# A decoder trunk on one core: first chunks made one by one, half of the last head's filler blocks put behind its values, first parts of the last feed-forward sooner

## The chip, the cores and the metric

The kernel runs on one core of a Trainium2 chip. The time is device microseconds (us) of one execution, the median of three runs. The engines have short names in the profile: PE (TensorE, matrix products), DVE (VectorE), ACT (ScalarE), POOL (GpSimd), SP (SyncE, which here only starts transfers). Each works through its own list of instructions in order, and they wait for each other by semaphores.

## The reference

Sequence 1024, model width 1024, one gated-convolution layer with a feed-forward, a shared compressed K/V, and one latent-attention layer (8 heads) with a feed-forward:

```python
h = h + short_conv_mixer(rms_norm(h, conv_norm_g[i]), conv_w_in[i], conv_w[i], conv_w_out[i])
h = h + swiglu_ffn(rms_norm(h, conv_ffn_norm_g[i]), conv_ffn_w13[i], conv_ffn_w2[i])
...
k_nope, k_pe, v = shared_mla_kv(h, kv_norm_g, w_dkv, kv_latent_norm_g, w_ukv, cos, sin)
...
p = jax.nn.softmax(jnp.where(mask, sc, neg), axis=-1).astype(v.dtype)
return jnp.einsum('bhqk,bkhd->bqhd', p, v)          # causal, in blocks of 128 queries
...
return attn.reshape(b, s, N_HEADS * V_HEAD_DIM) @ w_o
...
return rms_norm(h, final_norm_g)
```

## The kernel before

**Products.** Each float32 operand is split into a rounded high part (a cast on ACT, `split`, L111) and the rest (a subtraction on DVE or POOL, L112). A product is then three matmuls: high by high, high by low, low by high (`three`, L153 to L155; `gemm`, L146 to L150). So whatever PE multiplies has first passed one ACT and one DVE instruction.

**Order.** The convolution and both feed-forwards are written as steps of PE (`Steps`): `before(n, fn)` puts `fn` ahead of step n in the text, and the engines keep that order. The attention is written as plain code; there the Tile framework's scheduler sets each engine's order when the program is built, out of its own estimates.

**Start.** `first_x` loads four blocks of the input, transposes them raw, makes the norm, scales the first 512 columns (`scaled`, L919 and L921), and makes the operand of the first product: four chunks of 128 input columns by 512 tokens. `first_halves` makes chunks 0 and 1 (transposes, eviction with the gain at L952 and L954, split), `first_block(0, 1)` makes chunks 2 and 3 as one tile of 1024 columns: evictions at L932 and L934, one cast (L316), one subtraction (L317). Then the engines store the last raw block (L904), split the second weight (L378, L382) and scale the other columns; PE's first product (12 matmuls `q`) is followed by 16 transposes of those other columns.

**Attention.** For each head, eight `scores` blocks of 128 queries (PE `ps_s`, then on DVE the mask and the maximum, L1470 to L1473, on ACT the exponential, L1476, on DVE the division, L1478), and twice `pv`: transposes `ps_t` of p, their split into `pt` (L111, L112), and the values `ps_pv` (L1500 to L1502). The second `pv` of a head is kept in `pend` until the next head's blocks. PSUM holds two tiles of two banks (`ps2`, for `ps_s` and `ps_wo`) and four of one (`ps1`).

**Filler.** Between the scores of heads 0 to 6 PE makes the next head's keys and queries. Head 7 has no next head; there `project_o(O0, 0, (n,))` is put in, for n = 0 to 7: the output projection of the first five heads for one block of 128 output columns, 30 matmuls `ps_wo`. A block loads its weights (`wo_raw`, SP), splits them (`wo_hi` on ACT, `wo_lo` on POOL), loads the stream `h` from memory (L1549), and adds (L1552, DVE), which frees its `ps2` tile. `per` says after which pair of scores each block is written: two blocks after each pair. The last three heads' weights (`wo_r`, L1567) and their split (`wo_h`, `wo_l`) belong to the product that follows.

**Last feed-forward.** `Plain` adds heads 5 to 7 (`pl`, then `h` at L597). `Boundary.first(steps, n, at)` makes the norm of the first 512 tokens and, at the four steps of `at`, the first four operand parts (`Operand.first`, `block`: two instructions L301). Each call of `Operand.advance` moves the earlier parts one stage on: cast (L316), then subtraction (L317). `up(steps, quads2, bd.op, ahead)` makes the products `q`; `ahead` says how many steps sooner than usual the first two weights are split (L378, L382).

Of the kernel before, what the change touches and what calls it, by code (L numbers as in the profile page):

```python
# [9 lines left out]
F32 = mybir.dt.float32  # L10
F32R = mybir.dt.float32r
I32 = mybir.dt.int32
AF = mybir.ActivationFunctionType
ALU = mybir.AluOpType
AX = mybir.AxisListType

P = 128
S = 1024
D = 1024
KD = D // P  # L20
# [28 lines left out]
def trunk(ctx, tc, aps, out):  # L49
    nc = tc.nc  # L50
# [6 lines left out]
    def enter(name):  # L57

        if "stack" in phase:
            phase["stack"].close()  # L60
        phase["stack"] = ExitStack()
        phase["pool"] = phase["stack"].enter_context(tc.tile_pool(name=name, bufs=1, reuse_waits="tile"))
# [13 lines left out]
    def slot(name, dt=F32, shape=None):  # L76
        return slots.tile(shape or [P, S], dt, name=name, tag="act", bufs=NSLOT)
# [24 lines left out]
    def ps1(name):  # L102
        return phase["psum"].tile([P, 512], F32, name=name, tag="ps1", bufs=phase["ps"][1])
# [5 lines left out]
    def split(hi, lo, src, gain=None, eng=None):  # L109
        if gain is None:  # L110
            nc.scalar.copy(out=hi, in_=src)  # L111
            (eng or nc.vector).tensor_tensor(lo, src, hi.bitcast(F32), ALU.subtract)  # L112
        else:
            nc.scalar.activation(hi, src, AF.Copy, scale=gain)
            nc.vector.scalar_tensor_tensor(lo, src, gain, hi.bitcast(F32), ALU.mult, ALU.subtract)
# [42 lines left out]
    ident = const.tile([P, P], F32, name="ident")  # L158
# [25 lines left out]
    def gcol(nm, k):  # L184
        return vec[:, col[nm] + k:col[nm] + k + 1]
# [170 lines left out]
    class Quad:  # L356
# [88 lines left out]
        def evict(self, name):  # L445

            b = self.bank[name]
            add = lambda o, a: nc.vector.tensor_tensor(o, b, a, ALU.add)  # L448
            if name == 1:
                self.C1 = work("c1")  # L450
                nc.scalar.copy(out=self.C1[:, 512:], in_=b)
            elif name == 2 and name in self.onto:
                nc.scalar.activation(self.C1[:, :512], b, self.first)
            elif name == 2:
                add(self.C1[:, :512], self.C1[:, 512:])
                if self.first != AF.Copy:
                    nc.scalar.activation(self.C1[:, :512], self.C1[:, :512], self.first)
            elif name == 5:
                self.C2 = work("c2")
                nc.scalar.activation(self.C2[:, :512], b, AF.Copy, scale=-1.0)  # L460
                if 6 not in self.onto:
                    nc.vector.tensor_tensor(self.C1[:, 512:], self.C1[:, 512:], b, ALU.subtract)
            elif name == 6:
                nc.vector.tensor_tensor(self.C1[:, 512:], self.C1[:, 512:], b, ALU.subtract)
            elif name == 7:
                nc.vector.scalar_tensor_tensor(self.C2[:, 512:], b, -1.0, self.C1[:, 512:], ALU.mult, ALU.subtract)
                nc.vector.tensor_tensor(self.C2[:, :512], self.C2[:, :512], self.C2[:, 512:], ALU.add)
            elif name == 4:
                nc.vector.tensor_tensor(self.C2[:, :512], self.C2[:, :512], b, ALU.subtract)
            else:  # L470
                add(self.C1[:, 512:], self.C1[:, 512:])
                if self.first != AF.Copy:
                    nc.scalar.activation(self.C1[:, 512:], self.C1[:, 512:], self.first)  # L473
# [381 lines left out]
    steps = Steps()  # L855
    xt = [None] * KD
    xop = Operand("conv_norm_g")
# [80 lines left out]
    def first_block(f, kk):  # L938
        xop.part((f, 0), kk, block(f, 0, kk, nc.vector))
        xop.advance()  # L940

    def first_halves():

        b, hi, lo = slot("xraw"), slot("xh", F32R), slot("xl", F32R)
        pts = [ps1("xps") for _ in range(2)]
        for c, pt in enumerate(pts):
            for tb in range(4):
                nc.tensor.transpose(pt[:, tb * P:(tb + 1) * P], xt[tb][:, c * P:(c + 1) * P], ident)
        for c, pt in enumerate(pts):
            o = slice(c * 512, (c + 1) * 512)  # L950
            if c == 0:
                nc.vector.tensor_scalar(b[:, o], pt, gcol("conv_norm_g", c), None, ALU.mult)  # L952
            else:
                nc.scalar.activation(b[:, o], pt, AF.Copy, scale=gcol("conv_norm_g", c))  # L954
            split(hi[:, o], lo[:, o], b[:, o])
        xop.raw.setdefault((0, 0), {})[0] = b
        xop.X.setdefault((0, 0), {})[0] = (hi, lo)

    def first_x():
        for tb in range(3):  # L960
            raw_x(tb)
        squares(*range(4))
        last = raw_turn(3)
        gains(0)
        norms(0)
        conv_quads[0].pair_hi()
        scaled(0, slice(0, 512))
        conv_quads[0].pair_lo()
        first_halves()
        first_block(0, 1)  # L970
        xop.advance()
        raw_store(3, last, (nc.vector, nc.scalar))
        conv_quads[1].pair_hi()
        scaled(0, slice(512, S))
        conv_quads[1].pair_lo()
# [105 lines left out]
    quads2 = ffn_quads(A["mla_ffn_w13"], md["f2"])  # L1081
# [6 lines left out]
    n0 = len(steps.pe)  # L1088
# [392 lines left out]
    def pv(V, g, ps_, h):  # L1481

        nb = 4 * g + 4
        o = ps1("ps_pv")
        PT = {}

        def turn(kb):
            c = slice(max(kb - 4 * g, 0) * P, 512)
            t = ps1("ps_t")
            for j in range(c.start // P, 4):  # L1490
                nc.tensor.transpose(t[:, j * P:(j + 1) * P], ps_[j][:, kb * P:(kb + 1) * P], ident)  # L1491
            pt = hi_tile("pt")
            PT[kb] = pt[:, :512], pt[:, 512:]
            split(PT[kb][0][:, c], PT[kb][1][:, c], t[:, c])

        def product(kb):
            c = slice(max(kb - 4 * g, 0) * P, 512)
            vh, vl = [t[:, kb % 4 * 256 + h % 2 * P:kb % 4 * 256 + h % 2 * P + P] for t in V[kb // 4]]
            th, tl = [t[:, c] for t in PT[kb]]
            nc.tensor.matmul(o[:, c], lhsT=vh, rhs=th, start=kb == 0, stop=False)  # L1500
            nc.tensor.matmul(o[:, c], lhsT=vh, rhs=tl, start=False, stop=False)
            nc.tensor.matmul(o[:, c], lhsT=vl, rhs=th, start=False, stop=kb == nb - 1)  # L1502

        for kb in range(nb + 2):
            if kb < nb:
                turn(kb)
            if kb >= 2:
                product(kb - 2)
        gs = slice(g * 512, (g + 1) * 512)
        if h in Od:  # L1510
            split(Od[h][0][:, gs], Od[h][1][:, gs], o)
            return
        oh, ol = (pslot("oh", "oh", 1, F32R, [P, 512]), pslot("ol", "ol", 1, F32R, [P, 512]))
        split(oh, ol, o)
        move(od[h, 0, :, gs], oh)
        move(od[h, 1, :, gs], ol)
# [57 lines left out]
    for h in range(H):  # L1574
        if h >= 6:
            Od[h] = (tmp("oth", dt=F32R), tmp("otl", dt=F32R))
        if h + 1 < H:
            jobs = [lambda h=h: make_k(h + 1), lambda h=h: make_q(h + 1)]
            if h % 2:
                jobs = [lambda: make_qr(h + 1), lambda: make_v(h + 1)] + jobs  # L1580
        else:
            O1 = [load_o(5, r_(), r_())] + [Od[6], Od[7]]
            jobs = [lambda n=n: project_o(O0, 0, (n,)) for n in range(KD)]
        if h == 0:
            jobs = [lambda: make_q(1)]
        per = {1: ((0,), (), (), ()), 2: ((), (0,), (1,), ()), 4: ((0,), (1,), (2,), (3,)), 8: ((0, 1), (2, 3), (4, 5), (6, 7))}[len(jobs)]
        p = []
        for i in range(4):
            if i == 2 and pend:
                pv(*pend.pop(0))  # L1590
            p += [scores(Kt[h], Qt[h], 2 * i + d) for d in range(2)]
            if i == 2:
                pv(Vt[h], 0, p[:4], h)
            if i == 3:
                pend.append((Vt[h], 1, p[4:], h))
            for j in per[i]:
                jobs[j]()
        if h == 6:
            r_ = lambda: slot("oth", F32R)
            O0 = [load_o(k, r_(), r_() if k < 3 else cq_tile(4 - k)) for k in range(5)]  # L1600
# [2 lines left out]
    wo_parts(5)  # L1603
    for u in pend:
        pv(*u)
    enter("ffn")
    enter_psum(0, 8)

# [4 lines left out]
        steps.before(j, lambda k=k: wo_parts(k))  # L1613
    pl = Plain(steps, None, [[5], [6], [7]], Kept(O1), bd.norm.add, wo_kept)
    e = pl.ends
    bd.first(steps, e[1] + 2, (e[1] + 4, e[1] + 5, e[1] + 7, e[1] + 8))
    bd.second(steps, e[3] + 1)
    n0 = up(steps, quads2, bd.op, 8)
    for j, fn in enumerate(sums):
        paced(steps, n0 + 2 + 13 * j // 4, fn)  # L1620

# [114 lines left out]
```

## Time and profile before

| | |
|---|---|
| median of three runs | 2098.05 us (2097.63 to 2100.79) |
| the profiled execution | 2095.82 us |
| its span in the trace | 2093.7 us |
| busy share of the span | PE 98%, DVE 70%, ACT 41%, POOL 13% |
| matmuls | 9542 |

The page says that PE is busy in 98% of the span. So the time is PE's own work plus the places where it waits, and only those places and the clock can give anything. They are read from PE's list of instructions in order of time, where a bracket holds the idle time ahead of an instruction and what ended it.

### The profile page before, as it was taken

What the parts mean: (1) busy time and instruction counts of PE and PEld (TensorE: products, weight loads), DVE (VectorE), ACT (ScalarE), POOL (GpSimd) and SP (SyncE); (2) the same over time, 40 slices, a digit from 0 to 9 for tenths busy, and PEclk for the clock granted to TensorE, in tenths of its full rate; (3) what the DMA queues carried; (4) which work ended last, traced back from release to release, by engine and by line L of the source; (5) the groups of instructions that cost most, each with busy time, mean ns of one, the idle gap of its engine ahead of it and who ended that gap; (6) DMA issues with size and microseconds to landing.
All of it is one profiled execution on the core that took longest, in us unless ns stands there. A gap on an engine that the chain in (4) does not pass through costs nothing.

```text
span 2093.7 us, 25560 instructions
## 1 busy us (share of the span) xinstructions
PE 2053.9 (98%) x9542; PEld 1704.7 (81%) x9542; DVE 1463.5 (70%) x2200; ACT 855.7 (41%) x1440; POOL 269.4 (13%) x388
## 2 busy tenths in 40 slices
PE   7999999999999999999999999989999999999998
PEld 6888888888888887787888888867888888888887
DVE  5996666787667668867577777437887666667556
ACT  7533433533333333354245455225433333333455
POOL 1111100121122110000023322101111111100000
PEclk9999999999999999999999999999999999999999
DMA  7355765596766586554232213425487565686553
GB/s 234 81 133 139 238 239 175 112 220 180 190 163 153 141 287 246 206 206 150 72 70 70 66 52 111 163 81 163 125 201 186 154 160 163 151 286 225 186 169 129
DMA packets 274316, 338.97 MB, mean 162 GB/s; under 512 B 18047, under 2 KB 177984, under 8 KB 273872
## 3 DMA queue, kind: packets, MB, share of 16 engines
q1 hardware_dynamic: 240144, 262.71, 38.8%
q0 software_dynamic: 33888, 74.56, 16.6%
q8 instruction: 74, 1.21, 0.2%
q14 instruction: 50, 0.41, 0.1%
q10 hardware_dynamic: 160, 0.07, 0.0%
HBM read 260.22 MB, written 126.35 MB: 185 GB/s over the span
## 4 chain that ended last, share of the span: by engine, by line
PE 88%; DVE 6%; ACT 2%; issue 2%; DMA 1%; DVEq 0%; SPq 0%; ACTq 0%
PE q L154 17%; PE q L155 17%; PE q L153 17%; PE dn L155 5%; PE dn L153 5%; PE dn L154 5%; PE ps_s L1469 4%; PE pl L153 2%; PE pl L155 2%; PE pl L154 2%; DVE wp_lo L112 1%; PE ps_t L1491 1%; PE ps_l L155 1%; PE ps_l L153 1%; PE ps_l L154 1%
## 5 line engine op out<-in xcount | busy, mean ns | idle before, releaser
L153 PE MATMUL q<-xh,w_hi 128*128 128x512 f32 x1568 | 612.4, 391 | 1.1 <-ACT xh L316 1.1
L154 PE MATMUL q<-xl,w_hi 128*128 128x512 f32 x1568 | 610.5, 389 | 2.3 <-DVE xl L317 2.1
L155 PE MATMUL q<-xh,w_lo 128*128 128x512 f32 x1568 | 610.4, 389 | 0.0
L154 PEld LDWEIGHTS q<-xl,w_hi 128*128 128x128 f32 x1568 | 294.4, 188 | 64.6 <-DVE xl L317 2.8
L153 PEld LDWEIGHTS q<-xh,w_hi 128*128 128x128 f32 x1568 | 294.3, 188 | 63.3 <-ACT xh L316 1.5
L155 PEld LDWEIGHTS q<-xh,w_lo 128*128 128x128 f32 x1568 | 294.3, 188 | 61.0
L112 DVE TENSOR_TENSOR w_lo<-wr,w_hi 128x512 fp32r<-128x512 f32 (+1 forms) x272 | 191.9, 705 | 199.3 <-ACT w_hi L111 197.5
L111 ACT CAST w_hi<-wr 128x512 fp32r<-128x512 f32 (+1 forms) x272 | 170.4, 630 | 293.5 <-DVE wr L390 191.2
L155 PE MATMUL dn<-mp_hi,wp_lo 128*128 128x512 f32 (+1 forms) x628 | 243.9, 388 | 2.6 <-DVE wp_lo L112 0.8
L153 PE MATMUL dn<-mp_hi,wp_hi 128*128 128x512 f32 (+1 forms) x628 | 242.9, 387 | 0.0
L154 PE MATMUL dn<-mp_lo,wp_hi 128*128 128x512 f32 (+1 forms) x628 | 242.0, 385 | 0.0
L1072 POOL COPY paced<-pace 128x1 f32<-128x1 f32 x128 | 75.1, 587 | 1020.4 <-ACT pace L1071 1020.4
L112 DVE TENSOR_TENSOR mp_lo<-m,mp_hi 128x1024 fp32r<-128x1024 f32 x84 | 95.2, 1134 | 120.4 <-ACT mp_hi L111 120.4
L111 ACT CAST mp_hi<-m 128x1024 fp32r<-128x1024 f32 x84 | 82.4, 980 | 221.7 <-PE dn L154 211.5
L155 PEld LDWEIGHTS dn<-mp_hi,wp_lo 128*128 128x128 f32 x628 | 117.9, 188 | 32.7 <-DVE wp_lo L112 9.6
L154 PEld LDWEIGHTS dn<-mp_lo,wp_hi 128*128 128x128 f32 x628 | 118.0, 188 | 23.6
L153 PEld LDWEIGHTS dn<-mp_hi,wp_hi 128*128 128x128 f32 x628 | 118.0, 188 | 23.0 <-DVE h L740 0.2
L112 DVE TENSOR_TENSOR wp_lo<-w,wp_hi 128x1024 fp32r<-128x1024 f32 x84 | 94.8, 1128 | 0.0
L111 ACT CAST wp_hi<-w 128x1024 fp32r<-128x1024 f32 x84 | 82.1, 977 | 0.0
L473 ACT ACTIVATE c<-c 128x512 f32<-128x512 f32 x44 | 27.8, 632 | 131.7 <-DVE c L448 131.7
L1476 ACT ACTIVATE p<-ps_s,mx,rq 128x128 f32<-128x128 f32 (+3 forms) x64 | 53.2, 833 | 55.3 <-DVE mx L1473 50.1
L382 DVE TENSOR_TENSOR w_lo<-wr,w_hi 128x1024 fp32r<-128x1024 f32 x56 | 68.2, 1218 | 7.9 <-ACT w_hi L378 7.9
(296 smaller groups left out, 3231.9 us busy)
## 6 DMA issues: line engine op xcount, KB each, us to landing
m<-md_f SPq DMA_DIRECT2D x70, 512.0 KB, 4.9
md_f<-c SPq DMA_DIRECT2D x110, 256.0 KB, 3.7
wr<-in_conv_ffn_w_dram SPq DMA_DIRECT2D x47, 512.0 KB, 6.3
wr<-in_mla_ffn_w_dram SPq DMA_DIRECT2D x47, 512.0 KB, 5.4
w<-mw_f SPq DMA_DIRECT2D x40, 512.0 KB, 3.9
h<-hd SPq DMA_DIRECT2D x32, 512.0 KB, 9.6
wr<-in_conv_w_in_dram SPq DMA_DIRECT2D x31, 512.0 KB, 5.7
mw_f<-in_conv_ffn_w_dram POOLq DMA_DIRECT2D x30, 512.0 KB, 7.7
```

The lines of the kernel that those rows point to most:

```text
L111: nc.scalar.copy(out=hi, in_=src)
L112: (eng or nc.vector).tensor_tensor(lo, src, hi.bitcast(F32), ALU.subtract)
L153: nc.tensor.matmul(ps, lhsT=wh, rhs=xh, start=st, stop=False, **more)
L154: nc.tensor.matmul(ps, lhsT=wh, rhs=xl, start=False, stop=False, **more)
L155: nc.tensor.matmul(ps, lhsT=wl, rhs=xh, start=False, stop=en, **more)
L382: nc.vector.tensor_tensor(lo, self.ra, hi.bitcast(F32), ALU.subtract)
L473: nc.scalar.activation(self.C1[:, 512:], self.C1[:, 512:], self.first)
L1072: nc.gpsimd.tensor_copy(b, a)
L1469: nc.tensor.matmul(ps[:, a:b], lhsT=q[:, qs], rhs=k[:, a:b], start=i == 0, stop=i == 4)
L1476: nc.scalar.activation(p[:, :kw], ps[:, :kw], AF.Exp, bias=mx, scale=rq[:, qb:qb + 1], accum_out=rsum)
L1491: nc.tensor.transpose(t[:, j * P:(j + 1) * P], ps_[j][:, kb * P:(kb + 1) * P], ident)
```

## The change

At the start, `first_chunks` takes the place of `first_halves` and `first_block(0, 1)`: all sixteen transposes first, then for each of four chunks an eviction, a cast and a subtraction of 512 columns, woven by hand. In head 7, `per` writes one block of the projection after each pair of scores, and the other four (n = 4 to 7) are written after the last values. In the last feed-forward, the four operand parts come at e[1] + 4, 4, 5, 7, with one more `advance` at e[1] + 6, and `ahead` is 10.

```diff
-    def first_halves():
-        b, hi, lo = slot("xraw"), slot("xh", F32R), slot("xl", F32R)
-        pts = [ps1("xps") for _ in range(2)]
...
+    def first_chunks():
+        pts, T = [], [[slot("xraw"), slot("xh", F32R), slot("xl", F32R)] for _ in range(2)]
+        at = lambda k: [t[:, k % 2 * 512:k % 2 * 512 + 512] for t in T[k // 2]]
+        for k in range(4):
+            pts.append(ps1("xps"))
             for tb in range(4):
+                nc.tensor.transpose(pts[k][:, tb * P:(tb + 1) * P], xt[tb][:, k * P:(k + 1) * P], ident)
...
+        for fn, k in ((evict, 0), (high, 0), (evict, 1), (low, 0), (high, 1), (evict, 2), (low, 1), (high, 2), (evict, 3),
+                      (low, 2), (high, 3), (low, 3)):
+            fn(k)
...
         conv_quads[0].pair_lo()
-        first_halves()
-        first_block(0, 1)
-        xop.advance()
+        first_chunks()
...
-        per = {..., 8: ((0, 1), (2, 3), (4, 5), (6, 7))}[len(jobs)]
+        per = {..., 8: ((0,), (1,), (2,), (3,))}[len(jobs)]
...
     for u in pend:
         pv(*u)
+    for j in range(4, KD):
+        jobs[j]()
...
-    bd.first(steps, e[1] + 2, (e[1] + 4, e[1] + 5, e[1] + 7, e[1] + 8))
+    bd.first(steps, e[1] + 2, (e[1] + 4, e[1] + 4, e[1] + 5, e[1] + 7))
+    steps.before(e[1] + 6, bd.op.advance)
...
-    n0 = up(steps, quads2, bd.op, 8)
+    n0 = up(steps, quads2, bd.op, 10)
```

`evict` uses DVE for even chunks and ACT for odd ones, `high` is the cast on ACT, `low` the subtraction on DVE.

**Start, ACT's list.** These are ACT's instructions from the scaled input (`xt`) to the next scaled input; `xps` are the transposed chunks, `xraw`, `xh`, `xl` the operand and its parts. Before, then after:

```order
L919 ACTIVATE xt<-xt,rs 128x512 x2
L111 CAST xh<-xraw 128x512
L954 ACTIVATE xraw<-xps,vec 128x512
L111 CAST xh<-xraw 128x512
L934 ACTIVATE xraw<-xps,vec 128x512
L316 CAST xh<-xraw 128x1024
L904 COPY xr<-xps 128x512
```

```order
L959 CAST xh<-xraw 128x512
L953 ACTIVATE xraw<-xps,vec 128x512
L959 CAST xh<-xraw 128x512 x2
L953 ACTIVATE xraw<-xps,vec 128x512
L959 CAST xh<-xraw 128x512
```

The cast of 1024 columns has become two of 512, and the one of chunk 2 stands ahead of the eviction of chunk 3.

**The last values, PE's list.** Before, the last head's values stood alone behind the last block of the projection, each waiting for the `pt` that ACT and DVE make from the transposes just ahead:

```order
L150 MATMUL ps_wo<-oth,wo_lo 128x512 x2
L1491 MATMUL ps_t<-ident,p 128x128 x3
L1500 MATMUL ps_pv<-pt,vh 128x512
L1501 MATMUL ps_pv<-pt,vh 128x512
L1502 MATMUL ps_pv<-pt,vl 128x512
L1491 MATMUL ps_t<-ident,p 128x128 x4
```

After, the last transposes stand ahead of block 4 of the projection, whose last rows and the first values are these:

```order
L146 MATMUL ps_wo<-oth,wo_hi 128x512 x2
L148 MATMUL ps_wo<-cq,wo_hi 128x512
L1511 MATMUL ps_pv<-pt,vh 128x512
L148 MATMUL ps_wo<-cq,wo_hi 128x512
L150 MATMUL ps_wo<-oth,wo_lo 128x512 x2
L1512 MATMUL ps_pv<-pt,vh 128x512
```

The values lie among the matmuls of the projection's blocks 4 to 6, and block 7 comes behind them all. On DVE, the last two score blocks of head 7 now read like this (mask, maximum `mx`, the split of `wo_l`, the scaled maximum for which ACT's exponential waits):

```order
L1481 TENSOR_TENSOR ps_s<-ps_s,cmask 128x128
L1483 TENSOR_REDUCE mx<-ps_s 128x1
L112 TENSOR_TENSOR wo_l<-wo_r,wo_h 128x1024
L1484 TENSOR_SCALAR mx<-mx,nrq 128x1
L1481 TENSOR_TENSOR ps_s<-ps_s,cmask 128x128
```

Before, that split stood behind the second of the two maxima. SP's list of loads for the same stretch, as the piece of the difference:

```order
-L127 DMA wo_raw<-in_mla_w_o_dram 128x5x128 x5
-L1549 DMA h<-hd 128x1024 x4
-L127 DMA wo_raw<-in_mla_w_o_dram 128x5x128 x3
+L127 DMA wo_raw<-in_mla_w_o_dram 128x5x128 x4
+L1578 DMA wo_r<-in_mla_w_o_dram 128x1024
+L1560 DMA h<-hd 128x1024 x2
+L1578 DMA wo_r<-in_mla_w_o_dram 128x1024 x2
+L1560 DMA h<-hd 128x1024 x5
+L127 DMA wo_raw<-in_mla_w_o_dram 128x5x128
```

The weights of blocks 4 to 7 of the projection, four loads in all, now stand behind loads of `h`: seven ahead of block 4's.

**The last feed-forward, DVE's list.** From the norm's diagonal (`dg`) on; `h<-h,pl` adds the projection. Before, then after:

```order
L597 TENSOR_TENSOR h<-h,pl 128x512
L301 SCALAR_TENSOR_TENSOR xraw<-h,vec,R_12067 128x512 x2
L597 TENSOR_TENSOR h<-h,pl 128x512 x2
L301 SCALAR_TENSOR_TENSOR xraw<-h,vec,R_12067 128x512 x2
L597 TENSOR_TENSOR h<-h,pl 128x512 x4
L317 TENSOR_TENSOR xl<-xraw,xh 128x1024
```

```order
L301 SCALAR_TENSOR_TENSOR xraw<-h,vec,R_12069 128x512 x4
L597 TENSOR_TENSOR h<-h,pl 128x512 x2
L317 TENSOR_TENSOR xl<-xraw,xh 128x1024
L301 SCALAR_TENSOR_TENSOR xraw<-h,vec,R_12069 128x512 x2
L597 TENSOR_TENSOR h<-h,pl 128x512 x2
L317 TENSOR_TENSOR xl<-xraw,xh 128x1024
```

The first two parts are made together, and the first `xl` comes behind three additions where it came behind seven.

## Rows read from the trace of the kernel before

**Rows 1.** Windows: stretch, its length, busy time of each engine, granted PE clock, DMA

```profile
40.00:1100.00 1060.00, 1055.86 (x4731) 869.69 (x4730) 770.75 (x1067) 413.99 (x684) 125.74 (x189) 1.00 0.59 169
1450.00:2094.00 644.00, 636.61 (x2879) 527.27 (x2878) 442.08 (x605) 254.74 (x405) 61.00 (x88) 1.00 0.61 178
```

**Rows 2.** Timeline of PE at the start: start, duration, instruction, idle before

```profile
19.85 0.50 PE L153 MATMUL q<-xh,w_hi 128*128 128x512 f32 x1 [1.06 <-ACT xh L316]
21.11 0.50 PE L154 MATMUL q<-xl,w_hi 128*128 128x512 f32 x1 [0.76 <-DVE xl L317]
...
22.39 1.91 PE L929 MATMUL xps<-ident,xt 128*128 128x128 f32 x16
```

**Rows 3.** Timeline of ACT at the start

```profile
16.66 0.62 ACT L111 CAST xh<-xraw 128x512 fp32r<-128x512 f32 x1
17.18 0.68 ACT L934 ACTIVATE xraw<-xps,vec 128x512 f32<-128x512 f32 x1
18.75 1.04 ACT L316 CAST xh<-xraw 128x1024 fp32r<-128x1024 f32 x1 [0.89 <-DVE xraw L932]
...
21.12 1.34 ACT L919 ACTIVATE xt<-xt,rs 128x512 f32<-128x512 f32 x2
```

**Rows 4.** Timeline of DVE at the start

```profile
16.07 0.69 DVE L112 TENSOR_TENSOR xl<-xraw,xh 128x512 fp32r<-128x512 f32 x1 [0.68 <-ACT xh L111]
...
17.92 0.74 DVE L932 TENSOR_SCALAR xraw<-xps,vec 128x512 f32<-128x512 f32 x1
```

**Rows 5.** Timeline of PE in the last head and behind it

```profile
1317.11 0.51 PE L1500 MATMUL ps_pv<-pt,vh 128*128 128x512 f32 x1 [0.83 <-ACT pt L111]
1317.95 0.53 PE L1501 MATMUL ps_pv<-pt,vh 128*128 128x512 f32 x1 [0.33 <-DVE pt L112]
...
1372.63 0.60 PE L1491 MATMUL ps_t<-ident,p 128*128 128x128 f32 x4
1375.84 0.73 PE L1469 MATMUL ps_s<-kh,qnh 128*128 128x512 f32 x2 [2.61 <-ACT p L1476]
...
1382.32 1.22 PE L146 MATMUL ps_wo<-oth,wo_hi 128*128 128x512 f32 x2 [3.59 <-DVE h L1552]
...
1385.05 0.70 PE L146 MATMUL ps_wo<-oth,wo_hi 128*128 128x512 f32 x2
...
1386.51 0.62 PE L146 MATMUL ps_wo<-oth,wo_hi 128*128 128x512 f32 x2
...
1398.36 0.50 PE L1500 MATMUL ps_pv<-pt,vh 128*128 128x512 f32 x1 [0.46 <-ACT pt L111]
1399.49 0.50 PE L1501 MATMUL ps_pv<-pt,vh 128*128 128x512 f32 x1 [0.63 <-DVE pt L112]
```

**Rows 6.** Timeline of DVE ahead of PE's longest wait

```profile
1379.92 1.22 DVE L112 TENSOR_TENSOR wo_l<-wo_r,wo_h 128x1024 fp32r<-128x1024 f32 x1
1381.05 1.22 DVE L1552 TENSOR_TENSOR h<-ps_wo,h 128x1024 f32<-128x1024 f32 x1
```

**Rows 7.** Windows around the two longest waits; the clock is third from the end

```profile
1374.00:1376.00 2.00, 0.16 (x1) 0.16 (x2) 0.64 (x3) 1.19 (x2) 0.00 (x0) 1.00 0.64 231
...
1382.00:1384.00 2.00, 1.68 (x4) 1.39 (x5) 1.74 (x5) 1.29 (x2) 0.00 (x0) 0.50 0.97 315
```

**Rows 8.** Tile `wo_raw`: durations in ns, its split, issue to landing in us

```profile
L111 ACT CAST wo_hi<-wo_raw x7: 727/729/730, 1298.6 to 1370.4; 128x640 fp32r<-128x640 f32 x7
L112 POOL TENSOR_TENSOR wo_lo<-wo_raw,wo_hi x7: 1562/1566/1571, 1299.4 to 1371.2; 128x640 fp32r<-128x640 f32 x7
...
DMA to landing us min/median/max: 3.0/3.1/3.8
```

**Rows 9.** Tile `h` from 1300 to 1400 us: issue to landing

```profile
DMA to landing us min/median/max: 3.3/4.5/10.6
```

**Rows 10.** Timeline of PE at the last feed-forward's first norm and first product

```profile
1425.63 1.95 PE L224 MATMUL sp<-ones,nsq 128*128 128x1 f32 x16 [0.81 <-DVE nsq L759]
...
1445.18 0.51 PE L154 MATMUL q<-xl,w_hi 128*128 128x512 f32 x1 [1.32 <-DVE xl L317]
```

More of the change, by code (lines that the diff above doesn't have):

```diff
@@ L940, in first_block, with evict, high, low @@
         xop.advance()
-    def first_halves():
-        b, hi, lo = slot("xraw"), slot("xh", F32R), slot("xl", F32R)
-        pts = [ps1("xps") for _ in range(2)]
-        for c, pt in enumerate(pts):
-            for tb in range(4):
[L948 to L952, printed above, removed]
-            else:
[L954 to L957, printed above, removed]
+    def first_chunks():
[3 more added lines that the diff above has]
+            pts.append(ps1("xps"))
+            for tb in range(4):
+                nc.tensor.transpose(pts[k][:, tb * P:(tb + 1) * P], xt[tb][:, k * P:(k + 1) * P], ident)
+        def evict(k):
+            if k % 2:
+                nc.scalar.activation(at(k)[0], pts[k], AF.Copy, scale=gcol("conv_norm_g", k))
+            else:
+                nc.vector.tensor_scalar(at(k)[0], pts[k], gcol("conv_norm_g", k), None, ALU.mult)
+        def high(k):
+            b, hi, lo = at(k)
+            nc.scalar.copy(out=hi, in_=b)
+        def low(k):
+            b, hi, lo = at(k)
+            nc.vector.tensor_tensor(lo, b, hi.bitcast(F32), ALU.subtract)
+        for fn, k in ((evict, 0), (high, 0), (evict, 1), (low, 0), (high, 1), (evict, 2), (low, 1), (high, 2), (evict, 3),
+                      (low, 2), (high, 3), (low, 3)):
+            fn(k)
+        for kk, (b, hi, lo) in enumerate(T):
+            xop.raw.setdefault((0, 0), {})[kk] = b
+            xop.X.setdefault((0, 0), {})[kk] = (hi, lo)
     def first_x():
@@ L1585, in trunk @@
             jobs = [lambda: make_q(1)]
-        per = {1: ((0,), (), (), ()), 2: ((), (0,), (1,), ()), 4: ((0,), (1,), (2,), (3,)), 8: ((0, 1), (2, 3), (4, 5), (6, 7))}[len(jobs)]
+        per = {1: ((0,), (), (), ()), 2: ((), (0,), (1,), ()), 4: ((0,), (1,), (2,), (3,)), 8: ((0,), (1,), (2,), (3,))}[len(jobs)]
         p = []
```

## Prediction

> **What bounds the kernel now.** I read the windows first. From 40 to 1100 us PE is busy for 1055.86 of 1060 us, and from 1450 us to the end for 636.61 of 644 us [rows 1]. Long stretches are PE's own work, so whatever is saved ahead of them arrives at the end, and nothing on another engine counts unless PE waits for it. Then I read PE's timeline, with the reader looking only at the brackets. They lie in three places, and the change touches all three: the start, where the first product waits for its operand [rows 2]; the last head and the values behind it [rows 5]; and the first norm and first product of the last feed-forward [rows 10]. Last I read what ACT and DVE did ahead of those brackets [rows 3, 4, 6].
>
> **The start.** Nothing is removed; one tile of 1024 columns becomes two chunks of 512. Before, the first product waits 1.06 us for the cast of chunks 2 and 3 and 0.76 for their subtraction [rows 2], since that cast begins only at 18.75, behind both evictions, with ACT idle for 0.89 us [rows 3]. After, DVE's eviction of chunk 2 follows its first subtraction (16.07 + 0.69 = 16.76, then 0.74: 17.50) [rows 4], ACT casts it to 18.12 (0.62), evicts chunk 3 to 18.80 (0.68) and casts it to 19.42 (0.62) [rows 3]. The single cast ended at 18.75 + 1.04 = 19.79. Back to back, rows on ACT overlap by about 0.1 us (16.66 + 0.62 = 17.28 against the next start at 17.18) [rows 3], so 19.2 is nearer: ACT is 0.6 us ahead. PE itself would be some 1.8 us ahead, but its next work is 16 transposes of columns that ACT still has to scale. ACT does that from 21.12 to 22.46 [rows 3], so 0.6 us sooner. Before, the transposes began at 22.39 [rows 2] and met the last scaled block at once; after, three of each four are done while PE waits for the fourth, which gives back another 0.1 to 0.3. I take **0.8 us**, by ACT's chain, which is the longest here; the ends are 0 (ACT's later work in this stretch decides alone) and 1.8 (PE's own two waits).
>
> The split itself costs: two casts of 0.62 against one of 1.04 are 0.2 us more on ACT [rows 3]. That is in the 0.6 above, since ACT had 0.89 us of idle time to pay it from. [...]
>
> **The last head.** Four blocks of 30 matmuls move from between the scores to behind them; PE's work stays the same, and the waits change. Gone are:
> - 2.61 us ahead of the last scores, which waited for the exponential of the block before them to free a PSUM tile [rows 5]. The other tile was held by block 5, whose addition came late. With one block less at each place, the last scores take the tile of block 2, whose addition is done by then.
> - 3.59 us ahead of block 6, which waited for that addition at 1381.05, itself behind a maximum and a split of 1.22 us on DVE [rows 5, 6].
> - 0.46 and 0.63 us ahead of the last values, and 0.83 and 0.33 us ahead of the values at 1317 [rows 5]. PE now has matmuls of the projection between the transposes and the values that need them: at 1317 eight of them, about 1.9 us, at the end most of block 4.
> - the slow clock behind the long wait. [...] The wait of 2.61 us left the clock at 1.00 in its window [rows 7], so shorter waits cost only themselves.
>
> New is a wait of block 3 for the tile that the same exponential frees. Before, the tile was free 3.21 us after the transposes began (1372.63 to 1375.84) [rows 5]. After, DVE has a split of 1.22 us between the maximum and its scaling (its size is in [rows 6]), so 4.4 us; PE fills 0.8 of them with six transposes (0.60 for four) and 2.4 with ten score matmuls (1.46 / 6 each) [rows 5]: **1.2 us** remain. Its ends are 0 (the split slips behind) and 2.4 (a second split gets in between).
>
> The four blocks' loads hide as follows. Block 4's weights stand on SP behind loads of `h` that wait until the last scores have read their tiles. From the middle of those scores PE still has about 1.2 + 1.2 + 7.3 (30 matmuls of 0.24) + 0.8 us, some 10.5, before block 4. Against it stand 1.2 us of issuing three loads, a landing that I put at 5 (3.1 alone, 4.5 the median of `h` in company [rows 8, 9]), 0.73 of cast and 1.57 on POOL [rows 8]: 8.5. So 2 us are spare; with the longest landing, 10.6 [rows 9], it would be 3.6 late. Blocks 5 to 7 have a block more each.
>
> Sum here: 2.61 + 3.59 + 0.46 + 0.63 + 0.83 + 0.33 + 1.27 − 1.2 = **8.5 us**.
>
> **The last feed-forward.** With `ahead` at 10, both splits of the first weights (1.22 us each, as the same shape in [rows 6]) leave the run of additions and squares that ends in the norm, or reach its very beginning; the norm's matmuls waited 0.81 us for the end of that run [rows 10], so this wait goes with 0.4 us to spare even if only one split is out of its way. The wait of 1.32 us is for the subtraction of the second part [rows 10]. That part is now made with the first, one step sooner, and the added `advance` takes its cast and subtraction one step further forward: two steps of nine matmuls at 0.24, about 4.3 us. The third and fourth parts are needed only by later products. Both waits go: **2.1 us**. The ends are 0.8 and 2.1. DVE does no more than before, only in another order.
>
> **Sum.** 0.8 + 8.5 + 2.1 = 11.4 us. The profiled execution took 2095.82 us for its span of 2093.7, so it would take 2084.4; the median stands 2.2 us above the profiled one, and 2098.05 − 11.4 gives **2086.7 us**.
>
> **The rivals.**
> 1. Block 4 is late: its loads queue behind the loads of `h`. For it: the list of SP, and landings of up to 10.6 us in company [rows 9]. Against it: 2 us to spare. It would cost 2 to 4 us: 2089 to 2091.
> 2. The waits only move: the scores still hang on mask, maximum, exponential, and PE, with four blocks less between them, waits for each. In the first three pairs of scores PE now has half the filler, 7.3 us less. For it: the 2.61 us [rows 5] show what a missing filler costs, and two more such waits give back 5.2: 2092. Against it: the first pairs have the transposes and values of head 6 and then of head 7 around them in PE's list as well.
> 3. The change does nothing that lasts: the start and the head come sooner, and the last feed-forward waits for weights that now load later, behind the projection's. It would need 7 us or more of such waits: 2094 to 2099. Against it: PE is busy 99% from 1450 on [rows 1], and the first weights were split far ahead of use.
> 4. Slower: ACT's list has the casts of blocks 4 and 5 ahead of the casts of the last `pt`. If those weights come late, ACT stands, and with it the values, the softmax's rest and the next splits. It decides from a landing about 16 us beyond the 2 spare: then the 11.4 are gone and 4 more. That is longer than any landing in [rows 8, 9]; 2102 or more.
>
> **How the numbers follow.** The forecast, with terms within their ends (2085 to 2089), has 0.64; rival 1 has 0.14, rival 2 0.10, rival 3 0.06, rival 4 0.03; the remaining 0.03 is for more than forecast (the start's 1.8 in full, no wait at block 3), 2083 to 2085. A range from 2083 to 2091.5 holds the forecast, the better end and rival 1, 0.81. A measurement of this kernel can tell some 0.2%, 4.2 us, from no change. Faster by more than that is below 2093.9: forecast, better end and rivals 1 and 2, 0.90 with a little of rival 2 lost; the same 0.07; slower 0.03.
>
> **What would show it.** Right: in PE's timeline no bracket at the last values and none over 2 us between 1300 us and the last feed-forward, one of about 1.2 ahead of block 3, the clock at 1.00 there, no wait at the norm (`sp`) or at the first `q`, and the first transposes of the second operand at the start some 0.7 us sooner. Wrong: a bracket ahead of `wo_hi` of block 4 or `wo_lo` behind it, brackets at `ps_s` in the first pairs of head 7, or waits of the first `q` for `w_hi`.

## The result, and the profile after

The changed kernel takes 2084.97 us in the median of four runs (2083.35 to 2086.14). The ratio of its runs to those of the kernel before is 0.9928 (95% interval 0.9916 to 0.9940): 15.1 us faster (12.6 to 17.6) of 2098. The medians on record stand 12.9 us apart (2097.88 in four runs of the kernel before). The forecast was faster by 11.4 us, with 0.9 for its sign. The sign held, and the waits went where the forecast put them; the size did not hold: 2098.05 times the ratio is 2082.9, just below the range, though the median itself lies in it. The profiled execution took 2084.46 us for a span of 2082.7, 11.0 us less than the span of before; so the two profiles agree with the forecast, and the timed runs do not. That is the riddle that the experiments take up.

The long stretches are unchanged, as in [rows 1]. Windows of the kernel after:

```profile
40.00:1100.00 1060.00, 1055.98 (x4731) 869.66 (x4730) 770.52 (x1067) 414.09 (x684) 126.98 (x189) 1.00 0.59 169
1300.00:1395.00 95.00, 91.94 (x466) 76.74 (x465) 47.68 (x91) 32.87 (x61) 15.86 (x18) 1.00 0.46 153
...
1439.00:2083.00 644.00, 635.24 (x2872) 525.76 (x2870) 441.57 (x605) 253.28 (x403) 57.46 (x88) 1.00 0.61 178
```

PE's timeline of the kernel after, at the start, in the last head and at the last feed-forward (start, duration, instruction, idle before):

```profile
13.09 0.67 PE L949 MATMUL xps<-ident,xt 128*128 128x128 f32 x3 [2.20 <-DVE xt L921]
...
19.84 0.50 PE L154 MATMUL q<-xl,w_hi 128*128 128x512 f32 x1 [0.23 <-DVE xl L963]
...
20.84 0.77 PE L929 MATMUL xps<-ident,xt 128*128 128x128 f32 x3 [0.26 <-DVE xt L921]
...
36.84 0.77 PE L929 MATMUL xps<-ident,xt 128*128 128x128 f32 x5 [0.50 <-ACT xt L919]
...
1304.74 0.39 PE L1512 MATMUL ps_pv<-pt,vh 128*128 128x256 f32 x1 [0.57 <-DVE pt L112]
...
1353.73 0.73 PE L146 MATMUL ps_wo<-oth,wo_hi 128*128 128x512 f32 x2 [1.42 <-ACT p L1487]
...
1394.91 0.39 PE L153 MATMUL pl<-oth,wo_h 128*128 128x512 f32 x1
...
1413.73 0.40 PE L155 MATMUL pl<-oth,wo_l 128*128 128x512 f32 x1
1413.96 1.84 PE L224 MATMUL sp<-ones,nsq 128*128 128x1 f32 x16
...
1430.31 0.39 PE L153 MATMUL q<-xh,w_hi 128*128 128x512 f32 x1
...
1436.26 0.50 PE L153 MATMUL q<-xh,w_hi 128*128 128x512 f32 x1 [0.35 <-ACT c L451]
```

Where [rows 5] had waits of 2.61, 3.59, 0.46, 0.63, 0.83 and 0.33 us, one of 1.42 ahead of block 3 is left (forecast 1.2). The waits of [rows 10] at `sp` and at the first `xl` are gone; one of 0.35 for ACT's eviction of `c` is new. At the start 1.06 and 0.76 [rows 2] have become a few of about 0.25.

DVE ahead of block 3's wait shows the cause that was forecast: the split of `wo_l` stands between the maximum and its scaling.

```profile
1349.75 1.09 DVE L1483 TENSOR_REDUCE mx<-ps_s 128x1 f32<-128x896 f32 x1
1351.05 1.23 DVE L112 TENSOR_TENSOR wo_l<-wo_r,wo_h 128x1024 fp32r<-128x1024 f32 x1 [0.21 <-PE ps_s L1480]
1352.19 0.21 DVE L1484 TENSOR_SCALAR mx<-mx,nrq 128x1 f32<-128x1 f32 x1
```

The tile `wo_raw` of the kernel after, from 1352 us on: the four late loads land in 5.4 to 6.5 us (forecast 5), and ACT stands 3.2 us for block 4's, but PE has no bracket there:

```profile
  ACT wo_hi L111: 3.2, 1
...
DMA to landing us min/median/max: 5.4/5.4/6.5
```

### The profile page after: what moved, and what is told of

Its sections match the earlier page's. It is cut to its first block, busy times and chain, and to the rows that moved or that the text cites. A ratio compares the mean times of both kernels' runs of the same rounds, so it can differ in the third digit from the quotient of the medians.

```text
span 2082.7 us, 25559 instructions
## 1 busy us (share of the span) xinstructions
PE 2050.6 (98%) x9542; PEld 1701.2 (82%) x9542; DVE 1463.8 (70%) x2201; ACT 855.4 (41%) x1441; POOL 267.4 (13%) x388
## 4 chain that ended last, share of the span: by engine, by line
PE 88%; DVE 6%; ACT 3%; issue 2%; DMA 2%; DVEq 0%; SPq 0%; ACTq 0%
PE q L153 16%; PE q L155 16%; PE q L154 16%; PE dn L155 5%; PE dn L154 5%; PE dn L153 5%; PE ps_s L1480 4%; PE pl L155 2%; PE pl L153 2%; PE pl L154 2%; PE ps_t L1502 1%; DVE wp_lo L112 1%; PE ps_l L155 1%; PE ps_l L153 1%; PE ps_l L154 1%
## 5 line engine op out<-in xcount | busy, mean ns | idle before, releaser
L382 DVE TENSOR_TENSOR w_lo<-wr,w_hi 128x1024 fp32r<-128x1024 f32 x56 | 68.3, 1219 | 12.9 <-ACT w_hi L378 7.9
```

Source lines behind the costliest of these rows:

```text
L382: nc.vector.tensor_tensor(lo, self.ra, hi.bitcast(F32), ALU.subtract)
```

## The experiments

Two theories. **Theory 1**: the gain is the waits of the profile at their own price, and the rest is spread. **Theory 2**: the kernel before loses more in most executions than in the one that was profiled, at places that the change takes away; the profile had a lucky execution.

Three stretches of PE's timeline are compared in every profile, each as the difference of two starts. *Start*: from the first transposes of the scaled input (13.09 above) to the five transposes with the bracket of 0.50 (36.84). *Head*: from the values at 1304.74 to the first `pl`. *Norm*: from the last `pl` ahead of the sums `sp` to the first `q`. The same rows of the kernel before, from the profile that the prediction read:

```profile
13.28 2.17 PE L948 MATMUL xps<-ident,xt 128*128 128x128 f32 x8 [2.19 <-DVE xt L921]
...
37.86 0.77 PE L929 MATMUL xps<-ident,xt 128*128 128x128 f32 x5 [0.50 <-ACT xt L919]
...
1305.79 0.39 PE L1501 MATMUL ps_pv<-pt,vh 128*128 128x256 f32 x1 [0.58 <-DVE pt L112]
...
1405.54 0.45 PE L153 MATMUL pl<-oth,wo_h 128*128 128x512 f32 x1
...
1424.43 0.39 PE L155 MATMUL pl<-oth,wo_l 128*128 128x512 f32 x1
...
1442.08 0.39 PE L153 MATMUL q<-xh,w_hi 128*128 128x512 f32 x1
```

| profile | start | head | norm | timed ratio to before |
|---|---|---|---|---|
| before, as predicted from | 24.58 | 99.75 | 17.65 | |
| before_look1 | 24.57 | 102.29 | 19.19 | |
| before_look2 | 24.52 | 102.76 | 19.19 | |
| before_look3 | 25.45 | 101.20 | 19.19 | |
| start_only | 23.75 | 101.22 | 20.85 | 1.0005 (0.9996 to 1.0014) |
| ffn_only | 24.59 | 99.64 | 16.57 | 0.9979 (0.9971 to 0.9988) |
| before_filled | 24.58 | 99.67 | 17.64 | 0.9990 (0.9981 to 0.9999) |
| before_filled_look | 25.37 | 99.77 | 19.22 | |
| head_only | 25.68 | 90.19 | 19.25 | 0.9949 (0.9937 to 0.9962) |
| head_only_look | 24.58 | 90.18 | 17.64 | |
| head_filled | 24.59 | 90.19 | 17.64 | 0.9949 (0.9937 to 0.9962) |
| head_filled_look | 26.32 | 90.18 | 17.65 | |
| head_ffn | 24.54 | 90.22 | 16.57 | 0.9927 (0.9915 to 0.9940) |
| ahead8 | 23.76 | 90.44 | 19.23 | 0.9941 (0.9927 to 0.9955) |
| after | 23.75 | 90.17 | 16.58 | 0.9928 (0.9916 to 0.9940) |
| after_again | 23.75 | 90.18 | 16.58 | 0.9926 (0.9913 to 0.9938) |
| wo5_later | 23.76 | 89.72 | 16.58 | 0.9926 (0.9913 to 0.9940) |

**after_again** is the changed kernel, unedited.

> The changed kernel once more, to settle the size of the gain: the profiled pair differs by 11.4 us, the ratio of the timed runs says 15.1 (12.6 to 17.6). Theory 1 (the gain is the waits and the slow clock of the forecast, the rest is spread between executions): a ratio of about 0.9945 (11.4 us), its interval reaching over 11.4. Theory 2 (the kernel before loses about 3.5 us more in most executions than in the profiled one, at a place that the change takes away): 0.9928 again, 14 to 16 us, with an interval that leaves 11.4 out.

The ratio is 0.9926, 15.5 us (13.0 to 18.3): 11.4 lies outside, so theory 1 falls and the riddle is real.

**start_only, head_only, ffn_only** are the kernel before with one part of the diff each: `first_chunks`; `per` and the loop over `jobs[j]`; `bd.first`, `advance` and `ahead`.

> The kernel before with the new start alone. Theory 1: 0.8 to 1.1 us faster (the second product began 0.9 us sooner in the profile of the changed kernel), a ratio of 0.9995 to 0.9996. Theory 2, if its place is the start (granted clock 0.50 from 14 to 16 us before, 1.00 after): 3 to 5 us, 0.9976 to 0.9986. The rival that the start only moves a wait: 1.0000.

> The kernel before with four blocks of the projection behind the last head's values, alone. Theory 1: 8.3 to 8.5 us faster (the forecast's sum, a wait of 1.4 us for block 3 where 1.2 was forecast), a ratio of 0.9960; no bracket over 2 us between 1300 and 1400 us. Theory 2, if its place is the last head (the wait for block 5's addition and the clock behind it vary): 11.5 to 12.5 us, 0.994 to 0.9945. The rival that the waits only move: 3 us, 0.9985.

> The kernel before with the last feed-forward's first parts sooner, alone. Theory 1: 2.1 us faster less a small wait ahead of the first product (0.35 in the changed kernel's profile): 1.8 to 2.1, a ratio of 0.9990; the brackets of 0.81 at sp and 1.32 at the first xl are gone. Rival: without the head's change DVE and ACT are still behind with the last values there, so that one of the two waits stays: 0.8 to 1.3 us.

The head alone gave 10.7 us (8.0 to 13.2), with both answers to the question of size inside. The feed-forward gave 4.4 (2.5 to 6.1), more than its two waits. The start gave nothing in time (1.0 slower, from 2.9 slower to 0.8 faster), though its stretch is 0.8 shorter; one of its eleven runs took 2106.40, and by the medians it is 0.3 faster. This profile also has the longest norm.

**before_look1, before_look2, before_look3** are the kernel before, unedited.

> The kernel before again, for its profile: is the profiled execution of the prediction (sums sp to first q of the last feed-forward in 16.45 us, values at 1305.79 to first pl in 99.75) like the others? Theory 1: yes, both stretches within 0.2 us. Theory 2 (the clock falls behind the waits in most executions): sp to q 18.0 to 19.7, head 100 to 101.5 us.

> As before_look1, a second execution: by theory 1 the same figures as in the prediction's profile, by theory 2 at least one of the two stretches 1 us longer.

> A third further profile of the kernel before: stretch from the values at 1306 to the first pl 101 to 103 us and sp to q 18.0 or more by theory 2 (99.75 and 16.45 in the prediction's profile, which theory 1 takes as typical).

Theory 2 holds: heads 1.5 to 3.0 us longer (two of them beyond its 101.5) and norms 1.5 longer than in the profile behind the prediction. It is not a matter of the chip alone: start_only and ffn_only ran on one chip, with the same head, and read 101.22 and 99.64. PE's timeline of before_look1 shows how:

```profile
1376.04 1.22 PE L1469 MATMUL ps_s<-kh,qnh 128*128 128x512 f32 x2 [2.61 <-ACT p L1476]
1377.06 1.05 PE L1469 MATMUL ps_s<-kl,qnh 128*128 128x512 f32 x2
...
1383.95 1.22 PE L146 MATMUL ps_wo<-oth,wo_hi 128*128 128x512 f32 x2 [3.59 <-DVE h L1552]
...
1387.53 1.05 PE L148 MATMUL ps_wo<-oth,wo_hi 128*128 128x512 f32 x2
...
1428.47 1.95 PE L224 MATMUL sp<-ones,nsq 128*128 128x1 f32 x16 [0.81 <-DVE nsq L759]
...
1432.92 0.63 PE L153 MATMUL pl<-oth,wo_h 128*128 128x512 f32 x1
```

The waits are those of [rows 5, 10] to the hundredth; what differs is the work behind them. The last scores take 1.22 for two matmuls where [rows 5] have 0.73, and `pl` takes 0.63 where at a granted clock of 1.00 it takes 0.39. Windows of before_look1, the clock third from the end:

```profile
1376.00:1378.00 2.00, 1.96 (x5) 1.58 (x6) 0.85 (x2) 0.00 (x0) 0.00 (x0) 0.50 0.03 10
...
1386.00:1388.00 2.00, 2.00 (x7) 1.52 (x6) 0.33 (x1) 0.00 (x0) 0.00 (x0) 0.50 0.72 198
...
1432.00:1434.00 2.00, 2.00 (x6) 1.53 (x5) 0.58 (x1) 0.00 (x0) 0.00 (x0) 0.56 0.04 8
```

The granted clock is at 0.50 behind the first wait (0.71 from 1378 to 1380), at 0.50 from 1384 to 1388 behind the second (0.65 in the 2 us after), and at 0.56 behind the third.

**head_filled** and **before_filled** leave the late operands as they are and give PE needless work in the waits, whose products nobody reads. The other engines' lists of instructions are unchanged.

```diff
         sp = ps1("sp")
+        for _ in range(fills[0]):      # 3 at the last norm, else 0
+            nc.tensor.matmul(sp[:, :P], lhsT=ones, rhs=ones, start=True, stop=True)
...
+                if n == 6:             # before_filled alone
+                    dum = ps1("dum")
+                    for k in range(4):
+                        three(dum, hi[:, k, c], lo[:, k, c], O[k][0][:, :512], O[k][1][:, :512], k == 0, k == 3)
```

> The last head's part alone, and three matmuls of 128 columns on constants (about 0.25 us each) on PE just ahead of the norm's sums sp, in the time in which PE waits there for 0.81 us. No result is touched, and the data that sp waits for comes no sooner. Theory 2 (the last feed-forward's part gained 4.4 us where its two waits are 2.1, because the clock falls behind the idle time at the norm): the granted clock stays at 1.00 behind the norm, and the kernel gains 1.5 to 2.5 us over head_only, a ratio of 0.9938 to 0.9942. Theory 1 (the rest is spread): no gain over head_only, 0.9949; if the three matmuls end behind the norm's data, up to 0.2 us slower.

> head_only once more, for its profile: the wait at sp is there (0.81). Theory 2: sp to first q again 18 or more with the granted clock under 1.00 behind it; theory 1: 16.4.

> head_filled once more, for its profile: PE busy with three matmuls on constants in the wait at sp. Theory 2: sp to first q 16.4 at a clock of 1.00, as in its first profile (16.41); theory 1 has no reason for any difference from head_only.

At the norm this is not settled. Both profiles with filler have a granted clock of 1.00 there (norms of 17.64 and 17.65), but so has the second one of head_only without it (1.00, 17.64), and in time the filler gave nothing: the expected 1.5 to 2.5 us were missed. The mean clock of the five timed runs is 0.998 with the filler and without it.

> The kernel before with needless work on PE in two of its waits, and nothing sooner: twelve matmuls of 512 columns (2.7 us) into an unused PSUM tile ahead of the last scores, where PE waits 2.61 us, and three on constants ahead of the sums sp. If the clock falls because PE stands idle there: granted clock 1.00 behind the last scores (1376 to 1380 us) and behind the norm, the stretch from the values at 1306 to the first pl 99.5 to 101 us in place of 102.3 and 102.8, sp to q 16.4; in time 2 to 4 us faster than before, 0.9981 to 0.9990, with more work on PE. If idle time costs only itself (theory 1): no faster, up to 0.5 us slower, 1.0000 to 1.0002.

> A second profile of before_filled: if idle time is the cause, the clock is 1.00 behind both filled waits again; the wait of 3.59 us, which is not filled, may still have a fall of the clock behind it.

In the head the evidence is firmer. The last scores start 0.13 us sooner than in [rows 5] (1375.71 for 1375.84), and at a granted clock of 1.00. PE and windows of before_filled:

```profile
1374.90 0.39 PE L155 MATMUL dum<-oth,wo_lo 128*128 128x512 f32 x1
1375.14 0.82 PE L1496 MATMUL ps_t<-ident,p 128*128 128x128 f32 x6
1375.71 0.71 PE L1474 MATMUL ps_s<-kh,qnh 128*128 128x512 f32 x2
```

```profile
1376.00:1378.00 2.00, 2.00 (x10) 1.64 (x9) 0.46 (x1) 0.64 (x1) 0.00 (x0) 1.00 0.11 18
...
1382.00:1384.00 2.00, 1.85 (x4) 1.49 (x5) 1.74 (x5) 1.30 (x2) 0.00 (x0) 0.51 0.80 264
```

Both heads with filler are at 99.7 and 99.8, the unfilled wait of 3.59 still has its fall of the clock (0.51 above, 0.50 in the second profile), and the kernel is 2.1 us faster (0.2 to 4.0) with more work on PE; the exponential that the last scores need comes at most 0.4 us sooner, so most of the 2.1 is not its doing. The two heads alone would prove little, since two of six without filler are as short (99.75 and 99.64). But the mean granted clock lies between 0.996 and 0.999 in the eleven timed runs, 0.9975 in the mean, and between 0.994 and 0.998 in the fifteen runs of the kernel before beside them, 0.9957 in the mean: with work in these waits the clock is low less often. In the second profile with filler the clock at the norm fell to 0.50 all the same (19.22), with the filler in its wait.

**ahead8** and **head_ffn** undo one part each of the changed kernel: `up(steps, quads2, bd.op, 8)`, and the old start.

> The changed kernel with the first two weights of the last feed-forward split at the old step (8 in place of 10); the parts stay sooner. Theory 1: the wait of 0.81 us at sp is back and nothing else: 0.8 us slower than the changed kernel, a ratio of 0.9930. Theory 2: with the wait comes the fall of the clock, 2.5 to 3.5 us slower, 0.9938 to 0.9943. The rival that the earlier parts alone give all of it: no difference, 0.9926.

> The changed kernel with the start of before: the last head's and the last feed-forward's parts together. Theory 1 (each wait costs itself, the start is worth 0.8 to 1.0 us): 14.3 to 14.7 us faster than before, as the changed kernel's 15.3 less the start's term, a ratio of 0.9930 to 0.9932. Theory 2 (at the start too the granted clock falls to 0.50 for some us in most executions, and only the old start has that): 12.5 to 13.5 us, 0.9936 to 0.9940. The rival that the start gives nothing that lasts: as the changed kernel, 0.9926.

With `ahead` at 8 the wait of 0.81 is back and the norm is 2.65 us longer (19.23 against 16.58); in time it is 3.1 us by the ratios of ahead8 and after_again, whose intervals overlap. Without the new start nothing is lost that can be measured, again; an interval of 2.6 us to either side could not show 0.8.

**wo5_later** writes the split of the first product weights behind block 5, which puts the scaling ahead of the subtraction on DVE.

```diff
-    wo_parts(5)
     for u in pend:
         pv(*u)
     for j in range(4, KD):
+        if j == 6:
+            wo_parts(5)
         jobs[j]()
```

> The changed kernel with the split of the product's first weights written three blocks later, so that on DVE the scaled maximum of the next to last scores stands ahead of the subtraction wo_l of 1.23 us, not behind it. Theory 1: the wait of 1.42 us ahead of block 3 shrinks to 0 to 0.3, 1.1 to 1.4 us faster than the changed kernel, a ratio of 0.9919 to 0.9921. Rival: the subtraction only passes its time on to the next scaling or to the first addition, and the wait comes back one block later: no difference, 0.9926.

The wait shrank from 1.42 to 0.87, not to the expected 0 to 0.3. The scaling does stand ahead of the subtraction on DVE now, but ACT had begun the cast of `wo_h` when it ended, and the exponential came behind that cast. DVE, ACT and PE of wo5_later:

```profile
1352.02 0.21 DVE L1484 TENSOR_SCALAR mx<-mx,nrq 128x1 f32<-128x1 f32 x1
```

```profile
1352.13 1.05 ACT L111 CAST wo_h<-wo_r 128x1024 fp32r<-128x1024 f32 x1 [5.40 <-PE ps_s L1480]
1353.09 1.09 ACT L1487 ACTIVATE p<-ps_s,mx,rq 128x896 f32<-128x896 f32 x1
```

```profile
1354.32 0.73 PE L146 MATMUL ps_wo<-oth,wo_hi 128*128 128x512 f32 x2 [0.87 <-ACT p L1487]
```

The head is 0.46 us shorter, the time not measurably so.

## Why the prediction was right about the waits and short in size

- **Start, 0.8.** The stretch shrank from 24.58 to 23.75: 0.83, and 23.75 stands in all five profiles with the new start; with the old one it is 24.5 to 24.6 in eight of twelve and 25.4 to 26.3 in four. In these four the sixteen transposes behind the first product's two waits took 3.10 to 3.50 us, in the other eight 1.91; with the new start the same sixteen take 0.76 to 0.77 and 1.64 in two pieces in all five. In before_look3 the granted clock was 0.50 from 22 to 24 us; PE's row and that window stand below. The means, 24.95 and 23.75, are 1.2 apart, 0.4 more than the forecast. The forecast's chain over ACT is there: ACT's scaling of the second columns, counted from the first transposes, comes 0.5 us sooner (forecast 0.6). None of this is shown in time, in start_only or in head_ffn.

```profile
22.33 3.33 PE L929 MATMUL xps<-ident,xt 128*128 128x128 f32 x16
```

```profile
22.00:24.00 2.00, 2.00 (x10) 1.80 (x9) 1.89 (x3) 0.79 (x2) 0.80 (x1) 0.50 1.21 292
```

- **Last head, 8.5.** The waits went as said, and the new one came (1.42 for 1.2). Between the two first profiles the head shrank by 9.58. What was missing there is the price of a wait: the bracket is not all of it. From the last `pl` to `sp` it is 0.23 us without a wait and 1.20 with a bracket of 0.81, so 0.16 more than the bracket, as the matmul ahead (0.39 long, 0.23 apart) no longer overlaps the next; from `sp` on another 0.10 (16.45 against 16.35). If each wait in the head costs the same 0.26, which was read at the norm alone, five waits fewer are 1.3: 8.45 − 1.42 + 1.27 + 1.3 = 9.6.
- **The step that failed** is "The wait of 2.61 us left the clock at 1.00 in its window [rows 7], so shorter waits cost only themselves". It made one execution's clock into a rule, and so the sum had the slow clock as one term of 1.27 us in the head (from 1382.32 six matmuls in 2.73 us, the next six in 1.46 [rows 5], with a granted clock of 0.50 from 1382 to 1384 [rows 7]) and as nothing at the norm. In two of the three further profiles the last scores run at 0.50 (1.00 in before_look3); behind block 5's addition the clock is low for longer in all three (in before_look3 0.50 from 1384 to 1390, while the profile behind the prediction is at 0.70 from 1384 to 1386 and at 1.00 after); and behind the wait of 0.81 at the norm matmuls `pl` slow to 0.63 in six of eight profiles of kernels that have this wait unfilled (a granted clock of 0.50 from 1422 to 1424 in head_only), and in none of the five without the wait. The six profiles with the old head and no filler have a mean of 101.1, so the head is worth 11.0 and not 8.5; 1.4 of that is the clock beyond the 1.27. At the norm it is another 1.3.
- **Last feed-forward, 2.1.** Both waits went, one of 0.35 came. Between profiles with a granted clock of 1.00 there that is 1.07 at the norm and 0.94 over the first 41 matmuls of `q` (10.69 against 9.75). The seven profiles of unfilled kernels with the old feed-forward and `ahead` have norms of 18.99 in the mean, against 16.58: 2.4 and 0.94, so 3.4.
- **The sum** with these means is 1.2 + 11.0 + 3.4 = 15.6 us, or 15.2 with the start at 0.8, against 15.1 and 15.5 measured. Between the two first profiles the three stretches and the 41 matmuls shrank by 12.4, since that of before has no fall at the scores or the norm. They differ by only 11.0 because that of after lost time again elsewhere, 1.05 us of it at its very end, where the last eight stores took 6.30 us on SP's queue against 5.25. That the first pair comes so close to the 11.4 is luck.
- **The rivals.** Block 4 was not late for PE. The brackets in the first pairs of head 7 are those of before (0.57 and 0.75 against 0.58 and 0.75). The first `q` does not wait for weights. ACT stood 3.2 us for `wo_raw`, and the slower case needed some 18.

What stays open: why the start's 0.8 us does not show in time, why the clock falls in some executions and not in others, and why the filler at the norm gave nothing.

## What to carry to other kernels

A wait on PE was worth more than its bracket here: 0.26 us beyond it, read at one wait, and 1.5 to 3 us more in a stretch where the clock is low behind it. Whether it is low differs between executions of one program, so two or three profiles are needed before a stretch is priced; and the mean clock listed with each timed run (0.994 to 0.998 before, 0.998 to 1.000 after) is the first sign that a profile was not typical: the one that the prediction read has 0.998. To learn what a wait costs beyond itself, fill it with work that nobody needs and time that.

## What was not expected of the hardware

- In six of eight profiles matmuls slowed down behind a wait as short as 0.81 us and the sixteen matmuls of one column that follow it (1.95 us in before_look1): in before_look1 six matmuls then take 0.63 where others take 0.39, at a granted clock of 0.56 from 1432 to 1434.
- About 437 us a product `q` waits for ACT, and ACT for a store of the tile `c` that it is to write next. PE waited there between 0 and 1.79 us, with the old start and the new: that alone spreads executions by up to 1.8 us. In ffn_only the granted clock was 0.50 behind the wait of 1.79, and the way from the start's stretch to the head took 3.4 us longer there than in the first profile of before. PE in start_only, ACT in before_look2, and a window of ffn_only:

```profile
437.68 0.50 PE L153 MATMUL q<-xh,w_hi 128*128 128x512 f32 x1 [1.62 <-ACT c L460]
```

```profile
438.29 0.60 ACT L460 ACTIVATE c<-q 128x512 f32<-128x512 f32 x1 [3.74 <-DMA md_f<-c]
```

```profile
440.00:442.00 2.00, 2.00 (x6) 1.54 (x6) 1.86 (x4) 0.71 (x2) 0.35 (x1) 0.50 1.08 273
```
